# Attention scores by 64-row matmuls in pairs, with queries and keys stored whole and split on chip

## The chip, the core and the metric

One of the eight cores of a Trainium2 chip runs the whole program. The metric is the device time of one launch in microseconds. A core has a matrix engine (PE, with its weight loads, PEld, shown as an engine of their own), a vector engine (DVE), an activation engine (ACT), a general engine (POOL) and a queue that issues DMA transfers (SP). Each runs its own instructions in order and waits on semaphores for the others.

## What is computed

Two layers over a sequence of 1024 tokens of width 1024, everything in float32. Each layer is a norm, an input projection that also gives a gate, rotary embedding of queries and keys, attention, the gate, an output projection, a norm and a residual.

```python
# layer 0: three head groups of 16 heads of width 64, (window, dilation) = (128,1), (512,4), (2048,16)
qkv = (h @ w_in)[..., :n_qkv]; gate = (h @ w_in)[..., n_qkv:]
q, k = rope(q, pos), rope(k, pos)
o_g, lse_g = dilated_window_attention(q_g, k_g, v_g, window, dilation)     # for each group g
y = (sum_g softmax(lse)_g * o_g) * silu(gate) @ w_out
# layer 1: 8 heads, each with two query/key streams c of width 64 and values of width 128
s = einsum('bqhcd,bkhcd->bchqk', qblk, k) * scale                          # causal
p = softmax(s); a = p[:, 0] - lam * p[:, 1]; o = a @ v
y = (rmsnorm(o) * (1 - lambda_init)) * silu(gate) @ w_out
```

The contraction of every score, q times k, runs over the 64 elements of one head (or of one stream).

## The kernel before

**Numbers in two parts.** A float32 matrix x is held as xh (x rounded to the type float32r) and xl = x - xh. A product of two such matrices is made of xh·wh, xh·wl and xl·wh, three matmuls into one PSUM bank: `project` (L276) for the projections of queries, keys (tile `pqk`) and gates (`pg`), `v_block` (L213) for the values (`pv`), the loops of L386 and L443 for the output projection (`po`, `pe`). A PSUM bank holds 128 x 512 float32 numbers, and a matmul moves at most 512 columns.

**Order of the work.** PE takes its instructions in the order of the code. The other engines' orders are set by a scheduler from that. In each layer there is a stage that only projects, and then the attention stage. There the steps of the heads stand in a hand-made order, and a `Filler` runs matmuls of the projections between them: the remaining units of 128 queries and keys (`qk_unit`), then late gates and the first half of the output projection (`out_early`). In layer 0 the loop goes over 48 heads (8 pairs, 3 groups, 2 heads) of four steps c each: at step i come the scores of step i, the transposes of step i-3 (`tp`) and the products with the values of step i-5 (`up`), with the filler between them. In layer 1 the steps of 8 heads are sorted by due times.

**Queries and keys.** `qk_unit` projects a unit (two heads' queries and keys), applies the rotary embedding into two tiles `r`, splits each into `rh` and the rest in place (ACT rounds, POOL or DVE subtracts by `low`, L122), and stores both to DRAM (`qk_d`): four stores of 512 KB. `heads_in` then loads for one head `qh` and `ql`, each twice, into rows 0 to 63 and 64 to 127, and `ka`, whose upper 64 rows hold the keys' high part and whose lower 64 rows the low part. So one matmul over 128 rows gives qh·kh + qh·kl, and a second one ql·kh + ql·kl:

```python
for k, q in enumerate((qh, ql)):
    nc.tensor.matmul(sc[:, cols], lhsT=q[:, ts(b)], rhs=kv, start=k == 0, stop=k == 1)
```

In layer 0 (`Head.scores`, L602) step c takes the 128-query blocks 2c and 2c+1, four matmuls in one PSUM bank `sc`; a block has 128 or 256 keys. In group 0 block 0 has 128 keys and the seven others 256; in group 1 four blocks have 128 and four 256; in group 2 all have 128. In layer 1 (`DiffHead.scores`, L951) a step takes one stream s and one query block i with (i+1)·128 keys, in one or two spans of up to 512 columns, each with a bank of its own. The tag `s` of these banks has two buffers. DVE adds the mask and takes the minimum of a bank in one instruction (L609, L954), ACT takes the exponential (L612, L961). In layer 1 DVE then subtracts the second stream's probabilities from the first's (L970 to L973).

**Outputs of layer 0.** `product` adds up the values' products of four query blocks in a bank `up` (tag `u`, two buffers). When a half of the head is complete, at c = 1 and c = 3, `store` copies the lower 64 rows on ACT (`ul`, L680) and adds them to the upper ones on DVE (L685), which frees the bank. Group 2 uses `alone` instead, a bank a step.

**Loads.** In layer 0 a head's `load` (queries, keys and values `vt`) is called at c = 1 of the head before. All transfers are issued from one queue, SP, in order.

Of the kernel before, what the change touches and what calls it, by code (L numbers as in the profile page):

```python
# [18 lines left out]
P = 128  # L19
# [73 lines left out]
def trunk(ctx: ExitStack, tc: tile.TileContext, a: dict, out: bass.AP):  # L93
# [12 lines left out]
    qk_d = dram.tile([32, 2, 2, 2, 2, 32, T], F32, name="qk_d")  # L106
# [114 lines left out]
    def qk_unit(pool, unit, w, sub=1, on_pool=False):  # L221
# [7 lines left out]
        for c in range(2):  # L229
# [23 lines left out]
            latest[nc.gpsimd] = nc.gpsimd.tensor_add(put(r[1]), nat(t4), nat(t3)).ins  # L253
        written.add(unit)
        for e in range(2):
            rh = pool.tile([P, T], F32R, tag="rh", name="rh")
            nc.scalar.copy(rh, r[e])
            eng = nc.vector if on_pool or unit in (22, 23) else nc.gpsimd
            latest[eng] = low(eng, r[e].bitcast(F32R), r[e], rh).ins
            for i, t in enumerate((rh.bitcast(F32), r[e])):  # L260
                nc.sync.dma_start(qk_d[unit, :, :, i, e].rearrange("s h f t -> f (s h) t"), t)

    def heads_in(pool, unit, h):

        qh, ql, ka = (pool.tile([P, T], F32R, tag=t, name=t) for t in ("qh", "ql", "ka"))
        for t, e in ((qh, 0), (ql, 1)):
            for i in range(2):
                nc.sync.dma_start(
                    t[64 * i : 64 * i + 64].bitcast(F32), qk_d[unit, 0, h, e].rearrange("e f t -> (e f) t"))
        nc.sync.dma_start(ka.bitcast(F32), qk_d[unit, 1, h].rearrange("l e f t -> (l e f) t"))  # L270
        return qh, ql, ka
# [34 lines left out]
    def late_gates(pool, layer, w, fs, prepare):  # L306

        s = pool.tile([P, len(fs), T], F32, tag="r", name="sil", bufs=3 - layer)
        for v in gate_units(pool, layer, w, fs, None, prepare):
            if type(v) is tuple:  # L310
                f, c, o = v
                nc.scalar.copy(s[:, f - fs[0], ts(c, 512)], o)
            else:
                yield v
        nc.scalar.activation(s[:, : len(fs)], s[:, : len(fs)], AF.Silu)
        for i, f in enumerate(fs):
            nc.sync.dma_start(sil_d[layer][f], s[:, i])
            written.add(("gate", layer, f))
# [43 lines left out]
    r_bufs = {}  # L362
# [20 lines left out]
    def out_block(n, banks, kt, wh, wl, first, last):  # L383
        for c in range(2):
            for k, (l, r_) in enumerate(((XH, wh), (XH, wl), (XL, wh))):
                nc.tensor.matmul(  # L386
                    banks[c], lhsT=l[:, kt, ts(n)], rhs=r_[:, ts(c, 512)],
                    start=first and k == 0, stop=last and k == 2,
                )
                yield 512  # L390
# [23 lines left out]
    def out_weights(pool, w, kt):  # L414

        tags = {2: ("rh", "rh"), 4: ("qh", "ql"), 5: ("r", "r"), 6: ("ka", "ka")}
        if kt in tags:
            tiles = [pool.tile([P, D], F32 if t == "r" else F32R, tag=t, name="ow", bufs=2 if t != "r" else r_bufs[pool])
                     for t in tags[kt]]
            tiles = [t.bitcast(F32R) for t in tiles] if kt == 5 else tiles  # L420
        else:
            tiles = w_tiles([P, D])
        raw = raw_tile([P, D])
        nc.sync.dma_start(raw, w[ts(kt), :])
        split(*tiles, raw)
        return tiles

    def out_early(pool, layer, w, ws):

        ws[EARLY - 1] = out_weights(pool, w, EARLY - 1)  # L430
        for n in range(NB):
# [6 lines left out]
            for c in range(2):  # L438
                bank = ps.tile([P, 512], F32, tag="pj", name="pe")
                for kt in range(EARLY):  # L440
                    wh, wl = ws[kt]
                    for k, (l, r_) in enumerate(((XH, wh), (XH, wl), (XL, wh))):
                        nc.tensor.matmul(  # L443
                            bank, lhsT=l[:, kt, ts(n)], rhs=r_[:, ts(c, 512)],
# [109 lines left out]
    r_bufs[ep] = 3  # L554
    with tc.tile_pool(name="l0", bufs=2) as lp:
# [4 lines left out]
        class Head:  # L560
# [6 lines left out]
            def load(self):  # L567
                self.fin = heads_in(ep, NG * self.pr + self.g, self.h)
# [13 lines left out]

            def keys(self, b):
# [4 lines left out]
            def scores(self, c):  # L588

                qh, ql, ka = self.fin  # L590
                st = self.st
                sc = ps.tile([P, 512], F32, tag="s", name="sc")
# [542 lines left out]
```

## Time and profile before

| | |
|---|---|
| times of three runs | 1979.99, 1969.75, 1965.12 us; median 1969.75 us |
| the profiled execution | 1968.05 us, span 1966.1 us |
| layer 0, first to last score matmul | 426.6 to 1201.9 us of the span |
| layer 1, first to last score matmul | 1430.2 to 1864.6 us |
| bytes moved by DMA | 397.90 MB |
| matmuls | 10008, each with a weight load |

A row of the trace's timeline is start and length in us, engine, line, operation, output tile <- input tiles, stationary rows*columns, shape, count. A matmul's length is longer than the time until the next one starts, since matmuls are pipelined and their ends are modelled: what a matmul costs PE is the distance between starts. A weight load (PEld) belongs to the matmul that follows it.

### The profile page before, as it was taken

The page shows a single profiled execution, that of the slowest core. Times are in us where ns is not written, and L with a number is a line of the kernel's source. Part 1 is how long each engine was busy: PE and PEld are TensorE (multiplying, and loading weights), DVE is VectorE, ACT ScalarE, POOL GpSimd, SP SyncE. Part 2 cuts the span into 40 slices and gives each one's busy share as a digit, 9 for nine tenths or more (in the row PEclk, how much of TensorE's full clock was granted, in tenths as well). Part 3 has the DMA queues.
Part 4 walks back from the last instruction along what each step waited for, and adds up shares of the span by engine and source line. Part 5 has one row for each costly group of instructions (what it writes and reads, how often), then busy time and mean ns, then how long its engine had stood idle before and what let it go on. Part 6 is the DMA issues. An engine that isn't in the chain of part 4 may idle for free.

```text
span 1966.1 us, 29074 instructions
## 1 busy us (share of the span) xinstructions
PE 1885.2 (96%) x10008; PEld 1585.9 (81%) x10008; DVE 981.7 (50%) x2618; ACT 887.1 (45%) x2043; POOL 784.5 (40%) x553
## 2 busy tenths in 40 slices
PE   7999999999999999999999879999989899999897
PEld 5788888888888888888888757788878798887776
DVE  5311121135555555555555633650176778778726
ACT  4212112125656565656565645441244455556622
POOL 0000001154585857676776532320742435423201
PEclk9999999999999999999999989999999999999999
DMA  6424344277798989898989798442644565555843
GB/s 226 161 91 134 110 146 156 96 225 220 217 291 238 301 230 290 244 290 249 283 263 267 226 321 244 173 158 99 184 150 150 172 208 170 188 180 196 271 149 129
DMA packets 223683, 397.90 MB, mean 202 GB/s; under 512 B 40880, under 2 KB 131504, under 8 KB 223536
## 3 DMA queue, kind: packets, MB, share of 16 engines
q1 hardware_dynamic: 223536, 396.04, 64.2%
q8 instruction: 80, 1.31, 0.3%
q14 instruction: 67, 0.55, 0.1%
HBM read 254.87 MB, written 132.71 MB: 197 GB/s over the span
## 4 chain that ended last, share of the span: by engine, by line
PE 78%; DMA 8%; DVE 6%; ACT 2%; POOL 2%; issue 2%; SPq 1%; POOLq 0%; DVEq 0%; ACTq 0%
PE pqk L276 32%; PE pv L213 17%; PE pg L276 8%; PE po L386 4%; PE sc L602 4%; PE pe L443 3%; PE tp L625 3%; PE sc L951 3%; PE up L652 2%; PE ob L1004 2%; DMA ka<-qk_d 1%; PE tp L984 1%; DVE pm L954 1%; DVE pm L973 1%; DMA st_d<-st 1%
## 5 line engine op out<-in xcount | busy, mean ns | idle before, releaser
L276 PE MATMUL pqk<-XL,wh 128*128 128x512 f32 x1024 | 419.4, 410 | 0.0
L276 PE MATMUL pqk<-XH,wh 128*128 128x512 f32 x1024 | 408.7, 399 | 1.9 <-DVE t L252 1.9
L276 PE MATMUL pqk<-XH,wl 128*128 128x512 f32 x1024 | 409.6, 400 | 0.0
L122 POOL TENSOR_TENSOR wl<-raw,wh 128x1024 fp32r<-128x1024 f32 x59 | 141.8, 2404 | 511.2 <-ACT wh L184 507.2
L612 ACT ACTIVATE pm<-pm,st 128x128 f32<-128x128 f32 (+1 forms) x384 | 170.4, 444 | 153.1 <-DVE st L609 152.1
L276 PEld LDWEIGHTS pqk<-XH,wh 128*128 128x128 f32 x1024 | 193.7, 189 | 31.0 <-DVE t L252 2.7
L276 PEld LDWEIGHTS pqk<-XH,wl 128*128 128x128 f32 x1024 | 194.1, 190 | 27.1
L276 PEld LDWEIGHTS pqk<-XL,wh 128*128 128x128 f32 x1024 | 193.5, 189 | 27.2
L122 DVE TENSOR_TENSOR pp<-tp,pp 128x512 fp32r<-128x512 f32 (+2 forms) x192 | 104.2, 543 | 127.5 <-ACT pp L629 126.8
L184 ACT CAST wh<-raw 128x1024 fp32r<-128x1024 f32 x96 | 100.5, 1048 | 148.2 <-PE pqk L276 67.2
L213 PE MATMUL pv<-vwh,XH 128*128 128x512 f32 x384 | 153.1, 399 | 2.0 <-ACT XH L158 2.0
L213 PE MATMUL pv<-vwh,XL 128*128 128x512 f32 x384 | 153.0, 398 | 1.9 <-DVE XL L122 1.3
L213 PE MATMUL pv<-vwl,XH 128*128 128x512 f32 x384 | 152.3, 397 | 0.0
L961 ACT ACTIVATE pm<-pm,mx 128x256 f32<-128x256 f32 (+7 forms) x128 | 99.4, 776 | 115.1 <-DVE mx L960 60.2
L122 DVE TENSOR_TENSOR vs<-pv,vs 128x512 fp32r<-128x512 f32 x64 | 44.2, 691 | 202.2 <-ACT vs L517 196.2
L609 DVE CUSTOM_DVE_ANT_0 pm<-sc,masks 128x128 f32<-128x128 f32 (+1 forms) x384 | 119.2, 346 | 38.1 <-PE sc L602 37.1
L629 ACT CAST pp<-tp 128x512 fp32r<-128x512 f32 (+2 forms) x192 | 89.8, 468 | 79.4 <-PE up L652 57.9
L954 DVE CUSTOM_DVE_ANT_0 pm<-sc,md 128x512 f32<-128x512 f32 (+3 forms) x192 | 102.6, 551 | 34.4 <-PE sc L951 32.0
L251 POOL TENSOR_TENSOR r<-t 128x512 f32<-128x512 f32 x64 | 84.6, 1321 | 81.0 <-DVE t L250 79.8
L122 DVE TENSOR_TENSOR wl<-raw,wh 128x1024 fp32r<-128x1024 f32 x37 | 47.9, 1296 | 134.5 <-ACT wh L184 133.1
L517 ACT CAST vs<-pv 128x512 fp32r<-128x512 f32 x48 | 28.2, 586 | 187.8 <-PE pv L213 187.8
L602 PE MATMUL sc<-ka,qh 128*128 128x128 f32 (+1 forms) x384 | 95.3, 273 | 18.0 <-DMA ka<-qk_d 12.6
(514 smaller groups left out, 4430.2 us busy)
## 6 DMA issues: line engine op xcount, KB each, us to landing
qk_d<-rh SPq DMA_DIRECT2D x64, 512.0 KB
qk_d<-r SPq DMA_DIRECT2D x64, 512.0 KB
qh<-qk_d SPq DMA_DIRECT2D x128, 256.0 KB
ql<-qk_d SPq DMA_DIRECT2D x128, 256.0 KB
ka<-qk_d SPq DMA_DIRECT2D x64, 512.0 KB
v_d<-vs SPq DMA_DIRECT2D x48, 512.0 KB
raw<-in_dil_qk_dram SPq DMA_DIRECT2D x48, 512.0 KB
vt<-v_d SPq DMA_DIRECT2D x48, 512.0 KB
```

What stands on the lines that cost most here:

```text
L122: return eng.tensor_tensor(o, full, hi.bitcast(F32), ALU.subtract)
L184: nc.scalar.copy(wh, raw)
L213: nc.tensor.matmul(o, lhsT=l, rhs=r_, start=first and k == 0, stop=last and k == 3 * KT - 1, skip_group_check=True)
L251: nc.gpsimd.tensor_sub(put(r[0]), nat(t1), nat(t2))
L276: nc.tensor.matmul(o, lhsT=l[:, kt, :], rhs=r_[:, kt, tok], start=kt == 0 and k == 0, stop=kt == KT - 1 and k == 2)
L386: nc.tensor.matmul(banks[c], lhsT=l[:, kt, ts(n)], rhs=r_[:, ts(c, 512)], start=first and k == 0, stop=last and k == 2,)
L602: nc.tensor.matmul(sc[:, cols], lhsT=q[:, ts(b)], rhs=kv, start=k == 0, stop=k == 1)
L609: nc.vector.tensor_tensor_reduce(pm[:, cols], sc[:, cols], m[:, m.shape[1] - w_ :], 1.0, 3.0e38, ALU.add, ALU.min, st[:, 0, j : j + 1])
L612: nc.scalar.activation(pm[:, cols], pm[:, cols], AF.Exp, bias=st[:, 0, j : j + 1], scale=-1.0, accum_out=st[:, 1, j : j + 1])
L629: nc.scalar.copy(pp[:, 0, :w_], tp[:, :w_])
L954: nc.vector.tensor_tensor_reduce(pm[:, k0:k1], sc[:, :w_], m_, 1.0, 3.0e38, ALU.add, ALU.min, mx[:, j : j + 1])
L961: nc.scalar.activation(pm[:, :wq], pm[:, :wq], AF.Exp, bias=mx[:, 0:1], scale=-1.0, accum_out=den)
```

## The change

- **Storage.** `qk_unit` no longer splits. It stores the two tiles `r` as they are, two stores of 512 KB a unit.
- **Loads and splits.** In layer 0 `Head.load` loads one tile `qk` of 512 + 640 or 512 + 512 columns: rows 0 to 63 hold the first half of the head's queries and the keys that they need, rows 64 to 127 the second half and its keys. `Head.split` splits it into `qkh` and the rest in place (ACT, then POOL; DVE for the last two units). Load and split are called two heads ahead, at c = 0 and c = 2; the values are loaded one head ahead as before, by `load_values`. In layer 1 the keys `k` and two halves of the queries `q` hold stream 0 in rows 0 to 63 and stream 1 in rows 64 to 127, and are split on ACT and DVE.
- **Scores.** `row_tiled` issues three products, qh·kh, qh·kl, ql·kh, each as a pair of matmuls over 64 rows: one with rows 0 to 63 into one bank, one with rows 64 to 127 into the other. ql·kl is not computed. In layer 0 the pair is a block of the first and one of the second half of the head: step c takes blocks c and 7-c (group 0) or c and c+4. In layer 1 it is the two streams, a step is now one span of a query block for both, and the subtraction of the streams (`difference`) is put off until after the reductions of the next step.
- **Around it.** In layer 0 both halves of a head's output are complete at c = 3 only, so both stores come there; `ul` has two buffers. Tiles that later hold output weights, and the late gates' tiles, are cut anew.

```diff
+        for e in range(2):
+            nc.sync.dma_start(qk_d[unit, :, :, e].rearrange("s h f t -> f (s h) t"), r[e])
         written.add(unit)
-        for e in range(2):
-            rh = pool.tile([P, T], F32R, tag="rh", name="rh")
-            nc.scalar.copy(rh, r[e])
-            eng = nc.vector if on_pool or unit in (22, 23) else nc.gpsimd
-            latest[eng] = low(eng, r[e].bitcast(F32R), r[e], rh).ins
-            for i, t in enumerate((rh.bitcast(F32), r[e])):
-                nc.sync.dma_start(qk_d[unit, :, :, i, e].rearrange("s h f t -> f (s h) t"), t)
-
-    def heads_in(pool, unit, h):
-
-        qh, ql, ka = (pool.tile([P, T], F32R, tag=t, name=t) for t in ("qh", "ql", "ka"))
-        for t, e in ((qh, 0), (ql, 1)):
-            for i in range(2):
-                nc.sync.dma_start(
-                    t[64 * i : 64 * i + 64].bitcast(F32), qk_d[unit, 0, h, e].rearrange("e f t -> (e f) t"))
-        nc.sync.dma_start(ka.bitcast(F32), qk_d[unit, 1, h].rearrange("l e f t -> (l e f) t"))
-        return qh, ql, ka
+
+    def split_in_place(eng, hi, t):
+
+        nc.scalar.copy(hi, t.bitcast(F32))
+        low(eng, t, t.bitcast(F32), hi)
+
+    def row_tiled(outs, lq, rk):
+
+        for k, (i, j) in enumerate(((0, 0), (0, 1), (1, 0))):
+            for a, (o, q, kk) in enumerate(zip(outs, lq, rk)):
+                nc.tensor.matmul(o, lhsT=q[i], rhs=kk[j], start=k == 0, stop=k == 2)
...
             def load(self):
-                self.fin = heads_in(ep, NG * self.pr + self.g, self.h)
+
+                unit = NG * self.pr + self.g
+                self.n = 640 if self.g == 0 else 512
+                self.qk = ep.tile([P, QKW], F32R, tag="qk", name="qk", bufs=3)
+                for a in range(2):
+                    rows = self.qk[64 * a : 64 * a + 64].bitcast(F32)
+                    q, k = (qk_d[unit, s, self.h].rearrange("e f t -> (e f) t") for s in range(2))
+                    nc.sync.dma_start(rows[:, :512], q[:, ts(a, 512)])
+                    k0 = a * (T - self.n)
+                    nc.sync.dma_start(rows[:, 512 : 512 + self.n], k[:, k0 : k0 + self.n])
+
+            def split(self):
+                n = 512 + self.n
+                self.qkh = ep.tile([P, QKW], F32R, tag="qkh", name="qkh", bufs=3)
+                last = NG * self.pr + self.g in (22, 23)
+                split_in_place(nc.vector if last else nc.gpsimd, self.qkh[:, :n], self.qk[:, :n])
+
+            def load_values(self):
...
+            def blocks(self, c):
+
+                return c, 7 - c if self.g == 0 else c + 4
+
...
-                sc = ps.tile([P, 512], F32, tag="s", name="sc")
-                jobs = []
-                for b in (2 * c, 2 * c + 1):
+                jobs, ops = [], []
+                for a, b in enumerate(self.blocks(c)):
                     k0, nk = self.keys(b)
                     w_ = nk * P
-                    cols = slice(256 * (b % 2), 256 * (b % 2) + w_)
-                    kv = ka[:, k0 * P : k0 * P + w_]
-                    for k, q in enumerate((qh, ql)):
-                        nc.tensor.matmul(sc[:, cols], lhsT=q[:, ts(b)], rhs=kv, start=k == 0, stop=k == 1)
-                        cost += 256
+                    sc = ps.tile([P, 512], F32, tag="s", name="sc")
+                    rows = slice(64 * a, 64 * a + 64)
+                    at = 512 + k0 * P - a * (T - self.n)
+                    ops.append((sc[:, :w_], [t[rows, ts(b - 4 * a)] for t in (self.qkh, self.qk)],
+                                [t[rows, at : at + w_] for t in (self.qkh, self.qk)]))
+                    cost += 384
...
+                row_tiled(*zip(*ops))
+                for sc, cols, w_, j in jobs:
...
-                if c % 2:
-                    self.store(c // 2)
+                if c == 3:
+                    for half in range(2):
+                        self.store(half)
...
+        for hd in heads[:2]:
+            hd.load()
+            hd.split()
+        heads[0].load_values()
...
+                if i // 4 + 2 < len(heads):
+                    nxt = heads[i // 4 + 2]
+                    if c == 0:
+                        fill.until(NG * nxt.pr + nxt.g)
+                        nxt.load()
+                    if c == 2:
+                        nxt.split()
                 if c == 1 and i // 4 + 1 < len(heads):
-                    nxt = heads[i // 4 + 1]
-                    fill.until(NG * nxt.pr + nxt.g)
-                    nxt.load()
+                    heads[i // 4 + 1].load_values()
...
-            def load(self, part):
+            def load_keys(self):
                 fill.until(24 + self.h)
+                self.k = ep.tile([P, T], F32R, tag="k", name="k")
+                nc.sync.dma_start(self.k.bitcast(F32), qk_d[24 + self.h, 1].rearrange("h e f t -> (h e f) t"))
...
+            def split_keys(self):
+                self.kh = ep.tile([P, T], F32R, tag="kh", name="kh")
+                split_in_place(nc.vector, self.kh, self.k)
+
+            def load_queries(self, half):
+                t = ep.tile([P, 512], F32R, tag="q", name="q", bufs=3)
+                nc.sync.dma_start(
+                    t.bitcast(F32), qk_d[24 + self.h, 0].rearrange("h e f t -> (h e f) t")[:, ts(half, 512)])
+                self.q.append(t)
+
+            def split_queries(self, half):
+                self.qh.append(ep.tile([P, 512], F32R, tag="qh", name="qh", bufs=3))
+                split_in_place(nc.vector, self.qh[half], self.q[half])
...
+            def scores(self, i, j):
...
+                ops = []
+                for s in range(2):
+                    rows = slice(64 * s, 64 * s + 64)
                     sc = ps.tile([P, 512], F32, tag="s", name="sc")
-                    for k, q in enumerate((qh, ql)):
-                        nc.tensor.matmul(
-                            sc[:, :w_], lhsT=q[:, ts(i)], rhs=ka[:, k0:k1], start=k == 0, stop=k == 1)
-                    m_ = md[:, 640 - w_ :] if k1 == wq else md[:, :w_]
+                    ops.append((sc[:, :w_], [t[i // 4][rows, ts(i % 4)] for t in (self.qh, self.q)],
+                                [t[rows, k0:k1] for t in (self.kh, self.k)]))
+                row_tiled(*zip(*ops))
+                for s in range(2):
...
+                if later:
+                    later.pop()()
+                if j < len(spans) - 1:
+                    return
...
+                later.append(lambda: self.difference(i, wq, *pm, mx[1]))
+
+            def difference(self, i, wq, p0, p1, mx):
+
+                den, k = mx[:, 3:4], mx[:, 2:3]
+                nc.vector.reciprocal(den, den)
+                nc.vector.scalar_tensor_tensor(
+                    k, den, neg_lam, self.den[:, i : i + 1], ALU.mult, ALU.mult)
+                nc.vector.scalar_tensor_tensor(
+                    p0[:, :wq], p1[:, :wq], k, p0[:, :wq], ALU.mult, ALU.add)
...
-            for part in range(2):
-
-                due = h - 1 + SPAN * (NB * (NB - 1) + (part + 0.51) * NB) / 72
-                steps.append((due, lambda hd=hd, part=part: hd.load(part)))
+            for at, step in ((0.02, hd.load_keys), (0.04, lambda hd=hd: hd.load_queries(0)),
+                             (0.2, hd.split_keys), (0.22, lambda hd=hd: hd.split_queries(0)),
+                             (0.3, lambda hd=hd: hd.load_queries(1)), (0.5, lambda hd=hd: hd.split_queries(1)),
+                             (0.7, hd.load_values)):
+                steps.append((h - 1 + at, step))
-                for s in range(2):
-                    due = h + SPAN * (i * (i + 1) + (s + 0.5) * (i + 1)) / 72
-                    steps.append((due, lambda hd=hd, i=i, s=s: hd.scores(i, s)))
+                n = len(hd.spans(i))
+                for j in range(n):
+                    due = h + SPAN * (i + 1) * (i + 2 * (j + 0.25) / n) / 72
+                    steps.append((due, lambda hd=hd, i=i, j=j: hd.scores(i, j)))
+            steps.append((h + SPAN + 0.015, lambda: later and later.pop()()))
```

On PE, at the first score step of layer 0 (head 0 of group 0, blocks 0 and 1 before, 0 and 7 now), there stood:

```order
L276 MATMUL pqk<-XH,wl 128x512
L602 MATMUL sc<-ka,qh 128x128
L602 MATMUL sc<-ka,ql 128x128
L602 MATMUL sc<-ka,qh 128x256
L602 MATMUL sc<-ka,ql 128x256
L276 MATMUL pqk<-XH,wh 128x512
```

and now stands (`qkh` is the high part, `qk` the rest; queries and keys are in one tile):

```order
L272 MATMUL pqk<-XH,wl 128x512
L267 MATMUL sc<-qkh 128x128
L267 MATMUL sc<-qkh 128x256
L267 MATMUL sc<-qk,qkh 128x128
L267 MATMUL sc<-qk,qkh 128x256
L267 MATMUL sc<-qkh,qk 128x128
L267 MATMUL sc<-qkh,qk 128x256
L272 MATMUL pqk<-XH,wh 128x512
```

Four matmuls over 128 rows have become six over 64 rows, in alternating row halves; the filler's matmuls ahead and behind are the same.

On PE in layer 1, at query block 6 (896 keys, spans of 512 and 384 columns), before, where all four matmuls are of one stream:

```order
L951 MATMUL sc<-ka,qh 128x512
L951 MATMUL sc<-ka,ql 128x512
L951 MATMUL sc<-ka,qh 128x384
L951 MATMUL sc<-ka,ql 128x384
L213 MATMUL pv<-wh,XH 128x256
```

and now the step of its second span, for both streams:

```order
L267 MATMUL sc<-kh,qh 128x384 x2
L267 MATMUL sc<-k,qh 128x384 x2
L267 MATMUL sc<-kh,q 128x384 x2
L272 MATMUL pqk<-XH,wh 128x512
L272 MATMUL pqk<-XL,wh 128x512
```

Each row with x2 is a pair, the two streams in the two row halves; a step fills both banks of the tag `s` whatever its width.

On DVE in layer 0, where head 1 ends, before (L609 are the reductions of a score step, L122 with `pp` the split of transposed probabilities, L250 and L252 the rotary embedding, L685 the add of the store):

```order
L250 TENSOR_TENSOR t<-pqk,sin 128x512
L122 TENSOR_TENSOR pp<-tp,pp 128x384
L609 ISA pm,st<-sc,masks 128x128
L609 ISA st 128x1
L609 ISA pm,st<-sc,masks 128x256
L609 ISA st 128x1
L685 TENSOR_TENSOR u<-up,ul 64x512
L122 TENSOR_TENSOR pp<-tp,pp 128x384
L252 TENSOR_TENSOR t<-pqk,cos 128x512
```

and now, with the two adds L721 of one head (L644 are the reductions):

```order
L250 TENSOR_TENSOR t<-pqk,sin 128x512
L721 TENSOR_TENSOR u<-up,ul 64x512
L122 TENSOR_TENSOR pp<-tp,pp 128x256
L644 ISA pm,st<-sc,masks 128x256
L644 ISA st 128x1
L644 ISA pm,st<-sc,masks 128x256
L644 ISA st 128x1
L721 TENSOR_TENSOR u<-up,ul 64x512
L252 TENSOR_TENSOR t<-pqk,cos 128x512
```

The second add of a head now stands behind the reductions of the score step that follows the head's last product.

More of the change, by code (lines that the diff above doesn't have):

```diff
@@ L306, in late_gates @@
     def late_gates(pool, layer, w, fs, prepare):
[L308 to L312, printed above, removed]
-            else:
[L314 to L317, printed above, removed]
+        for f in fs:
+            if layer:
+                s = [pool.tile([P, 512], F32, tag="x", name="sil") for _ in range(2)]
+            else:
+                t = pool.tile([P, T], F32, tag="r", name="sil", bufs=3)
+                s = [t[:, ts(c, 512)] for c in range(2)]
+            for v in gate_units(pool, layer, w, (f,), None, prepare if f == fs[-1] else None):
+                if type(v) is tuple:
+                    nc.scalar.copy(s[v[1]], v[2])
+                else:
+                    yield v
+            for c in range(2):
+                nc.scalar.activation(s[c], s[c], AF.Silu)
+            for c in range(2):
+                nc.sync.dma_start(sil_d[layer][f, :, ts(c, 512)], s[c])
             written.add(("gate", layer, f))
@@ L414, in out_weights @@
     def out_weights(pool, w, kt):
[L416 to L422, printed above, removed]
+        spare = out_spare[pool].get(kt)
         raw = raw_tile([P, D])
         nc.sync.dma_start(raw, w[ts(kt), :])
-        split(*tiles, raw)
-        return tiles
+        halves = lambda t: [t[:, ts(c, 512)] for c in range(2)]
+        if spare is None or len(spare) == 1:
+            tiles = w_tiles([P, D]) if spare is None else spare[0]()
+            split(*tiles, raw)
+            return [halves(t) for t in tiles]
+        tiles = []
+        for c, new in enumerate(spare):
+            tiles.append(new())
+            split(*tiles[c], raw[:, ts(c, 512)])
+        return list(zip(*tiles))
     def out_early(pool, layer, w, ws):
@@ L620, in transposes @@
                 n = 0
-                for kb in (2 * c, 2 * c + 1):
+                for kb in self.blocks(c):
                     for b in (kb, kb + 1):
@@ L639, in product @@
                     self.up = [None, None]
[L642 removed]
+                for kb in self.blocks(c):
                     for half in range(2):
@@ new lines, in spans @@
+            @staticmethod
+            def spans(i):
+                wq = (i + 1) * P
+                cut = wq - max(256, wq - 512) if wq > 512 else 0
+                return [(0, cut), (cut, wq)] if cut else [(0, wq)]
+            def scores(self, i, j):
+                spans = self.spans(i)
+                wq = (i + 1) * P
+                if j == 0:
+                    self.now = (
+                        lp.tile([P, wq], F32, tag=f"pm0{i}", name="pm0", bufs=1),
+                        lp.tile([P, T], F32, tag="pm1", name="pm1"),
+                        [lp.tile([P, 4], F32, tag=f"mx{s}", name=f"mx{s}") for s in range(2)])
+                *pm, mx = self.now
+                k0, k1 = spans[j]
+                w_ = k1 - k0
+                m_ = md[:, 640 - w_ :] if k1 == wq else md[:, :w_]
+                ops = []
+                for s in range(2):
+                    rows = slice(64 * s, 64 * s + 64)
@@ L1066, in filler1 @@
             yield from out_early(ep, 1, a["diff_w_out"][0], held)
-        heads = [DiffHead(h) for h in range(8)]
+        heads, later = [DiffHead(h) for h in range(8)], []
         held = {}
```

108 lines of the change are left out of this document (48 added, 60 removed).

## The prediction

> **What bounds the kernel now.** I read the busy times first, then the same by stage, then single score steps in the timeline.
>
> ```profile
> PE 1885.2 (96%) x10008; PEld 1585.9 (81%) x10008; DVE 981.7 (50%) x2618; ACT 887.1 (45%) x2043; POOL 784.5 (40%) x553
> 1100.00:1190.00 90.00, 67.97 (x362) 56.23 (x360) 40.50 (x125) 48.34 (x125) 34.59 (x26) 0.89 0.91 274
> 440.00:1100.00 660.00, 658.81 (x3723) 562.63 (x3722) 368.15 (x1184) 388.47 (x1078) 449.17 (x312) 1.00 0.88 261
> 1420.00:1905.00 485.00, 457.00 (x2769) 400.06 (x2768) 348.77 (x953) 248.13 (x484) 178.04 (x120) 0.99 0.58 185
> ```
>
> Behind the colon stand the stretch's length, the busy time of PE, PEld, DVE, ACT and POOL, the granted clock, the DMA share and GB/s. PE leads with 96%. In 660 us of layer 0's attention it idles for 1.2 us, so whatever a score step saves or costs PE there is time of the kernel. Slack is in two places: the end of layer 0 (22 us of 90) and layer 1 (28 us of 485).
>
> A busy PE is not PE at its peak, so I look at what a score step occupies: a step of four 128-column matmuls, then one of four 256-column ones, then the 512 and 384 columns of layer 1.
>
> ```profile
> 880.01 0.22 PE L602 MATMUL sc<-ka,qh 128*128 128x128 f32 x1
> ...
> 880.13 0.19 PEld L602 LDWEIGHTS sc<-ka,qh 128*128 128x128 f32 x1
> 880.24 0.19 PEld L602 LDWEIGHTS sc<-ka,ql 128*128 128x128 f32 x1
> 880.35 0.19 PEld L276 LDWEIGHTS pqk<-XH,wh 128*128 128x128 f32 x1
> ...
> 880.69 0.39 PE L276 MATMUL pqk<-XL,wh 128*128 128x512 f32 x1
> 811.23 0.28 PE L602 MATMUL sc<-ka,qh 128*128 128x256 f32 x1
> ...
> 811.94 0.39 PE L276 MATMUL pqk<-XL,wh 128*128 128x512 f32 x1
> 1578.88 0.40 PE L951 MATMUL sc<-ka,ql 128*128 128x512 f32 x1
> 1579.11 0.34 PE L951 MATMUL sc<-ka,qh 128*128 128x384 f32 x1
> 1579.29 0.34 PE L951 MATMUL sc<-ka,ql 128*128 128x384 f32 x1
> ```
>
> A 512-column matmul holds PE for 0.23 us (1578.88 to 1579.11), a 384-column one for 0.18. The first step holds PE from 880.01 to 880.69 less the 0.23 of the 512-column matmul behind it, 0.45 us, the second in the same way 0.48. So a 256-column matmul costs 0.12, and a 128-column one hardly less, 0.11: there the weight loads set the pace, one every 0.11 us (880.13, 880.24, 880.35).
>
> **The scores, the main term.** How many there are, in layer 1 (layer 0 has 48 heads of 8 blocks):
>
> ```profile
> L951 PE MATMUL sc<-ka,qh x192: 221/386/687, 1430.2 to 1864.3; 128*128 128x512 f32 x80, 128*128 128x256 f32 x48, 128*128 128x384 f32 x48, 128*128 128x128 f32 x16
> ```
>
> By the masks, 16·(1+4+8) = 208 of layer 0's 384 blocks have 128 columns and 176 have 256, two matmuls each: 416·0.11 + 352·0.12 = 88 us. Layer 1 has the quoted row twice (for `qh` and `ql`): 160·0.23 + 96·0.18 + 96·0.12 + 32·0.11 = 69 us. Together 157 us of PE.
>
> The change makes six matmuls of four, 576 more in all, each over half the rows. If both of a pair run at once, loads included, a step takes three slots for four: 157/4 = **39 us less**. No row of this trace shows two matmuls at once; the ends are three slots (-39) and six (+78, nothing shared). I take three slots, since the two of a pair share neither rows, weights nor bank, and give what lies between to the rivals. The Trainium skill ("TensorEngine Tiling (Array Packing)", Key Properties) says that different tiles can load weights and multiply in parallel; no run here shows it yet.
>
> **Switching between full and half rows.** A step now switches PE into 64-row tiles and back: 288 steps, 576 switches. One operation of this kernel has a tile that isn't 128 by 128, the transposes `tps` with 32 columns:
>
> ```profile
> L691 PE MATMUL tps<-ident,st 128*32 128x128 f32 x8 | 2.2, 272 | 0.0
> 467.04 0.40 PE L276 MATMUL pqk<-XL,wh 128*128 128x512 f32 x1
> 467.04 0.10 PEld L691 LDWEIGHTS tps<-ident,st 128*32 128x32 f32 x1
> 467.27 0.27 PE L691 MATMUL tps<-ident,st 128*32 128x128 f32 x1
> 467.28 0.77 PEld L652 LDWEIGHTS up<-pp,vt 128*128 128x128 f32 x6
> ```
>
> Its load starts with the matmul before it, its matmul comes the usual 0.23 us later, and the six loads behind it take 0.77 - 0.19 = 0.58 us for five distances, 0.12 each. So this switch costs nothing, and I put 0 for the others. It is a narrower tile, though, not a shorter one. The upper end is what a matmul's modelled end lies behind its successor's start, 0.40 - 0.23 = 0.17 us: PE would have to run empty before it changes tiles, 576·0.17 = 98 us in all.
>
> The Trainium skill (same page and section) states a rule that speaks against this change: changing the tiling mode, not just the tile, drains TensorE. On `tps` the trace disagrees; by the rule the scores and switches together would come to about +59 us, by the row to -39.
>
> **The output banks of layer 0.** Both banks `up` of a head are now held until c = 3, and the next head's first product needs both. The add of one store of before, and the next head's products:
>
> ```profile
> 885.73 1.08 DVE L685 TENSOR_TENSOR u<-up,ul 64x512 f32<-64x512 f32 x1
> ...
> 886.55 0.57 PE L652 MATMUL up<-pp,vt 128*128 128x256 f32 x4
> ```
>
> The bank comes free at 886.81. That hurts nobody now, because the products of 886.55 go to the other bank. With two stores, and the second add behind the next step's reductions, the second bank would come free at 887.9 at the earliest, 1.1 us after the second block of that product wants it (886.55 + 0.23). Behind the waiting matmul stands all of PE. There are 32 heads of groups 0 and 1: 31 such places, 0 us where DVE is ahead, 34 where each is like this one. DVE is busy for 56% of this stretch and this place is one of its fuller ones by the order; I take a third, **+12 us**.
>
> **The score banks.** A step now takes both banks of tag `s`, so it waits for the reductions of the step before.
>
> ```profile
> 881.03 0.08 DVE L609 DVE_READ_ACCUMULATOR2_ANT st<- 128x1 f32 x1
> ...
> 884.03 0.22 PE L602 MATMUL sc<-ka,qh 128*128 128x128 f32 x1
> PE sc L951 <- DVE mx L954: 17.3, 14, 2.8
> ```
>
> In layer 0 the reductions are over 2.9 us before the next step's matmul: +3 us for those where DVE is late, up to +10. In layer 1 PE waits 17.3 us for these banks already. A step of two spans took both banks there too, and `difference` now stands behind the reductions instead of ahead of the next ones. I take 0, with ends of -17 (all gone) and +17 (twice as much).
>
> **The loads.** At the end of layer 0 the chain of waits runs through transfers:
>
> ```profile
> 1117.60 9.08 DMA vt<-v_d
> 1126.70 10.73 DMA XH<-y_d
> 1137.45 7.79 DMA wb<-wt_d
> 1145.26 8.62 DMA ka<-qk_d
> qk_d<-rh SPq DMA_DIRECT2D x64, 512.0 KB
> qk_d<-r SPq DMA_DIRECT2D x64, 512.0 KB
> qh<-qk_d SPq DMA_DIRECT2D x128, 256.0 KB
> ql<-qk_d SPq DMA_DIRECT2D x128, 256.0 KB
> ka<-qk_d SPq DMA_DIRECT2D x64, 512.0 KB
> ```
>
> SP issues in order, so the load of `ka` stands behind that of `wb`, which waits for its own data, and PE waits for `ka`. Queries and keys are now asked for two heads ahead, and their bytes fall from 64 + 96 MB (the five rows) to 32 + 34 MB, of 398 in all. Both work on the 22 idle us of that stretch; `vt` and `wb` stay as they were. I take **-12**, between 0 and -22.
>
> **Moved at no cost.** The splits keep their number of elements, but for 16 heads of 1152 columns:
>
> ```profile
> L122 POOL TENSOR_TENSOR r<-r,rh 128x1024 fp32r<-128x1024 f32 x44 | 105.5, 2406 | 4.7 <-ACT rh L257 4.7
> ```
>
> An eighth of 2.4 us more sixteen times is 5 us of POOL, busy for 449 of 660 us. The chain of store, load, ACT's rounding and POOL's 2.4 us is covered by two heads of four steps of some 4 us (880.01 to 884.03), 32 us. Without that cover, a late split stops PE for as long as it is late.
>
> **The sum.** -39 + 12 + 3 + 0 - 12 = -36. The profiled execution took 1968.05 us, 0.1% under the median of the runs shown, so 1932.
>
> **The rivals.**
> - *Loads one after another, matmuls at once.* If the two weight loads of a pair take turns at 0.11 us, a pair of up to 256 columns costs 0.22. The first pair's loads hide behind the 0.23 us matmul ahead, so a narrow step pays five loads, 0.55, instead of 0.45 or 0.48: 104·0.10 + 88·0.07 = +17 in layer 0. In layer 1 the 40 steps of 512 columns keep their gain (-0.23 each, -9), the 384-column ones gain 1 and the narrower ones lose 2: -8. That is +9 where I have -39: **1980**. For it: the loads are the pace already at 128 columns. Against it: a load fills only its own rows.
> - *A drain at each switch* (slower than before). PE runs empty ahead of the first half-row matmul of a step and again behind the last one. At 0.17 us for each of 576 switches: 1932 + 98 = **2030**. It decides the sign from 36/576 = 0.06 us a switch. Against it stands `tps`.
> - *No overlap at all*, six slots: the change doesn't do what it says. +78 for -39: **2049**. Against it: separate banks and rows.
>
> **Chances.** Forecast 0.55, with a range of its own from 1905 to 1962 by the ends of the banks and loads; loads in turn 0.18; drain 0.17 (from 0.05 to 0.17 us each, so 1961 to 2030); no overlap 0.07; something else 0.03. About 1% (20 us) is what a measurement of this kernel can tell from no change. Of the forecast's 0.55, 0.45 lies below 1950; the turns add 0.02 there: faster 0.47. Same: 0.10 of the forecast, 0.12 of the turns, 0.06 of a mild drain, 0.01: 0.29. The rest is slower, 0.24. The range runs from 1905 to 2025: it leaves out no overlap, the fuller half of the drain and a little below.
>
> **What would show it.** A pair's two matmuls starting within some hundredths of a microsecond, and a step of 128 columns holding PE for 0.33 us (right), 0.55 (loads in turn) or 0.67 (no overlap). A gap before the first half-row matmul and behind the last one (drain). PE's waits for L721 on `up` (banks), and none for queries and keys at the end of layer 0. I am wrong above all if one of the first three steps is.

## The result, and the profile after

The changed kernel takes 2068.01 us (median of four runs), the kernel before 1971.26 us: a ratio of 1.0492 with a 95% interval from 1.0461 to 1.0522. I had forecast 1932, with a range up to 2025. The profiled execution took 2067.73 us, its span 2065.9 us, 99.8 us more than before.

The engines' busy times from the page, and the stretches of the trace that the prediction showed of before (length, then PE, PEld, DVE, ACT and POOL, the granted clock, the DMA share, GB/s):

```profile
PE 1973.3 (96%) x10584; PEld 1560.3 (76%) x10584; DVE 996.6 (48%) x2626; ACT 896.0 (43%) x2061; POOL 779.4 (38%) x554
440.00:1100.00 660.00, 632.26 (x3570) 486.36 (x3568) 338.87 (x1044) 344.23 (x948) 397.90 (x273) 0.98 0.47 144
1100.00:1190.00 90.00, 86.56 (x492) 66.54 (x493) 45.35 (x139) 45.26 (x126) 55.00 (x38) 0.98 0.48 150
1420.00:1905.00 485.00, 468.03 (x2764) 380.17 (x2762) 295.62 (x793) 212.19 (x418) 185.88 (x129) 0.98 0.35 119
```

PE still has 96%, but in the 660 us of layer 0's attention it now idles for 28 us where it idled for 1.2, and the clock is 0.98. In those 660 us it does 3570 matmuls where it did 3723, though the program has 576 more: both the steps and the waits between them have grown. The stretch from 1100 to 1190 us no longer holds layer 0's end, which now comes at 1283.7 us; by the first and last score matmuls of the two traces layer 0 takes 856.9 us for 775.3, layer 1 453.4 for 434.4.

A score step of two 256-column blocks in the timeline:

```profile
889.85 0.39 PE L272 MATMUL pqk<-XL,wh 128*128 128x512 f32 x1
890.08 0.40 PE L272 MATMUL pqk<-XH,wl 128*128 128x512 f32 x1
890.40 0.19 PEld L267 LDWEIGHTS sc<-qkh 64*128 64x128 f32 x2 [0.36 <-issue]
890.40 0.39 PE L267 MATMUL sc<-qkh 64*128 64x256 f32 x2
890.63 0.28 PE L267 MATMUL sc<-qk,qkh 64*128 64x256 f32 x2
890.75 0.28 PE L267 MATMUL sc<-qkh,qk 64*128 64x256 f32 x2
890.96 0.19 PEld L272 LDWEIGHTS pqk<-XH,wh 128*128 128x128 f32 x1
890.96 0.50 PE L272 MATMUL pqk<-XH,wh 128*128 128x512 f32 x1
891.29 0.39 PE L272 MATMUL pqk<-XL,wh 128*128 128x512 f32 x1
```

Two things are to be seen. First, each row with x2 is a pair, and the second pair is gone after 0.12 us (890.63 to 890.75), which is what one 256-column matmul took before: the two of a pair do run at once. Second, four distances are too long by some 0.1 us each: the 512-column matmul ahead (890.08 to 890.40, 0.32 for 0.23), the first pair (0.23 for 0.12), the last pair (0.21 for 0.12) and the 512-column matmul behind (0.33 for 0.23). At both ends the weight load stands at the same time as its own matmul, where the load of an ordinary matmul starts with the matmul before it. From 890.08 to 891.29, less two times 0.23, the step holds PE for 0.75 us; before it was 0.48. By the median distances over all steps between 512-column matmuls it is 0.68 us at 128 columns, 0.75 at 256 and 1.10 at 512. Three slots of 0.11, 0.12 and 0.23 are 0.33, 0.36 and 0.70, so the two switches of a step cost 0.35 to 0.40 us whatever its width.

The waits of PE, those of ACT for the loaded tiles, and one of the seven changes of the head pair in the timeline, with the stretch behind it:

```profile
PE sc L267 <- DVE mx L1024: 16.7, 17, 3.2
PE sc L267 <- DVE st L644: 10.1, 9, 2.0
PE up L687 <- DVE us__7526 L708: 3.6, 1, 3.6
PE up L687 <- DVE u L721: 3.4, 4, 1.2
ACT qkh L260 <- DMA qk<-qk_d: 90.0, 44, 14.7
868.50 3.04 SPq L788 DMA_DIRECT2D wb<-wt_d  x5
871.64 0.54 SPq L587 DMA_DIRECT2D qk<-qk_d  x1
877.38 1.05 ACT L260 CAST qkh<-qk 128x1024 fp32r<-128x1024 f32 x1 [4.32 <-DMA qk<-qk_d]
881.18 0.37 ACT L707 COPY us__7526<-up 128x256 f32<-128x256 f32 x1
882.60 0.42 DVE L708 TENSOR_TENSOR us__7526<-us__7526,up 128x256 f32<-128x256 f32 x1
883.17 0.41 PE L687 MATMUL up<-pp,vt 128*128 128x128 f32 x2 [3.61 <-DVE us__7526 L708]
883.41 0.45 PE L272 MATMUL pqk<-XH,wl 128*128 128x512 f32 x1
884.04 0.63 PE L272 MATMUL pqk<-XL,wh 128*128 128x512 f32 x1
884.47 0.63 PE L272 MATMUL pqk<-XH,wl 128*128 128x512 f32 x1
883.00:887.00 4.00, 3.83 (x15) 2.66 (x16) 2.10 (x7) 1.81 (x6) 3.84 (x4) 0.60 0.42 125
```

SP issues the loads of `qk` behind five of `wb`; ACT comes to the split of that tile and stands 4.3 us for it, and the copy out of the output bank, which is behind it on ACT, comes at 881.18. DVE's add (L708), which needs the copy and frees the bank, comes at 882.60, and PE, which needs that bank, waits 3.6 us. The granted clock of the 4 us after that is 0.60, and matmuls of 512 columns are 0.43 us apart (884.04 to 884.47). The Trainium skill ("TensorE: Matmul & The Clock Gate", Part 1) says that an idle window of about 3.4 us halves the clock; the 0.60 agrees in kind. So such a wait costs more than its length. PE's list of waits has seven of this kind, 1.6 to 4.1 us each and 23.7 in all, one at each change of the pair; five of the other six also have a stretch of 3 to 7 us at a granted clock of 0.50 beside them.

### The profile page after: what moved, and what is told of

The parts are those of the page before. It is cut to its first block, busy times and chain, and to the rows that moved or that the text cites. A ratio compares the mean times of both kernels' runs of the same rounds, so it can differ in the third digit from the quotient of the medians.

```text
span 2065.9 us, 29927 instructions
## 1 busy us (share of the span) xinstructions
PE 1973.3 (96%) x10584; PEld 1560.3 (76%) x10584; DVE 996.6 (48%) x2626; ACT 896.0 (43%) x2061; POOL 779.4 (38%) x554
## 4 chain that ended last, share of the span: by engine, by line
PE 75%; DMA 8%; DVE 7%; ACT 4%; issue 2%; SPq 2%; POOL 2%; ACTq 0%; POOLq 0%; DVEq 0%
PE pqk L272 28%; PE pv L213 16%; PE pg L272 8%; PE sc L267 6%; PE po L387 4%; PE pe L446 3%; PE up L687 3%; PE tp L660 2%; DMA qk<-qk_d 2%; PE ob L1081 2%; PE tp L1061 1%; ACT pm L1036 1%; DMA qk_d<-r 1%; DMA st_d<-st 1%; ACT wh L184 1%
## 5 line engine op out<-in xcount | busy, mean ns | idle before, releaser
L272 PE MATMUL pqk<-XH,wh 128*128 128x512 f32 x1024 | 428.4, 418 | 0.0
L272 PE MATMUL pqk<-XL,wh 128*128 128x512 f32 x1024 | 425.1, 415 | 0.0
L122 POOL TENSOR_TENSOR wl<-raw,wh 128x1024 fp32r<-128x1024 f32 x60 | 143.7, 2395 | 466.3 <-ACT wh L184 465.8
L122 DVE TENSOR_TENSOR pp<-tp,pp 128x384 fp32r<-128x384 f32 (+2 forms) x192 | 104.3, 543 | 188.7 <-ACT pp L664 188.2
L122 POOL TENSOR_TENSOR qk<-qk,qkh 128x1024 fp32r<-128x1024 f32 (+1 forms) x44 | 109.6, 2493 | 111.1 <-ACT qkh L260 101.7
L122 DVE TENSOR_TENSOR vs<-pv,vs 128x512 fp32r<-128x512 f32 x64 | 44.1, 690 | 199.6 <-ACT vs L520 195.2
L644 DVE CUSTOM_DVE_ANT_0 pm<-sc,masks 128x128 f32<-128x128 f32 (+1 forms) x384 | 120.4, 347 | 22.9 <-PE sc L267 21.1
L664 ACT CAST pp<-tp 128x384 fp32r<-128x384 f32 (+2 forms) x192 | 89.6, 467 | 91.0 <-PE up L687 75.3
L687 PEld LDWEIGHTS up<-pp,vt 128*128 128x128 f32 x544 | 82.9, 192 | 41.3 <-issue 29.0
L1024 DVE CUSTOM_DVE_ANT_0 pm<-sc,md 128x512 f32<-128x512 f32 (+2 forms) x192 | 100.3, 550 | 27.0 <-PE sc L267 26.8
L687 PE MATMUL up<-pp,vt 128*128 128x256 f32 (+1 forms) x544 | 86.4, 280 | 27.1 <-DVE us__6322 L708 4.1
```

Source lines behind the costliest of these rows:

```text
L122: return eng.tensor_tensor(o, full, hi.bitcast(F32), ALU.subtract)
L272: nc.tensor.matmul(o, lhsT=l[:, kt, :], rhs=r_[:, kt, tok], start=kt == 0 and k == 0, stop=kt == KT - 1 and k == 2)
L644: nc.vector.tensor_tensor_reduce(pm[:, cols], sc, m[:, m.shape[1] - w_ :], 1.0, 3.0e38, ALU.add, ALU.min, st[:, 0, j : j + 1])
L664: nc.scalar.copy(pp[:, 0, :w_], tp[:, :w_])
L687: nc.tensor.matmul(self.up[half][:, (qs[0] - 4 * half) * P : (qs[-1] + 1 - 4 * half) * P], lhsT=self.vt[:, kb, :], rhs=self.parts[c][:, e, ...
L1024: nc.vector.tensor_tensor_reduce(pm[s][:, k0:k1], ops[s][0], m_, 1.0, 3.0e38, ALU.add, ALU.min, mx[s][:, j : j + 1])
```

## Experiments

All ratios are to the kernel before, timed beside each run.

**Are the splits late?** The split of a head was called a head later.

```diff
-                    if c == 2:
-                        nxt.split()
+                if c == 2 and 0 < i // 4 + 1 < len(heads) and i // 4 >= 1:
+                    heads[i // 4 + 1].split()
```

> Row tiling stays; a head's split moves from two heads ahead to one head ahead (c = 2), its loads stay where they are. Theory (a queue at each change of the head pair: the loads of queries and keys stand on SP behind the joint statistics, ACT reaches the split before they land and stands in order ahead of reductions and the copy that frees an output bank): the seven changes cost 6 to 8 us each beyond the other heads' 0.95 us, about 44 us in all, and go: 2068 - 44 = 2024. Rival (the two output banks, held until c = 3, stop PE there by themselves): the waits stay, 2060 to 2070.

Measured: 2078.22 us, ratio 1.0533 (1.0508 to 1.0558). My expectation failed, but the edit hadn't done what I took it for. ACT's wait is still there, and the trace has each split some 3 us behind the issue of its loads, as before the edit:

```profile
ACT qkh L260 <- DMA qk<-qk_d: 100.1, 46, 14.5
```

The scheduler, not the order of the code, places ACT's instructions. So this run decides nothing between the theories. The 10 us that it is slower than the change stay open; the order on DVE and ACT differs in many places.

The next run ties the split to an instruction of ACT:

```diff
-                    nc.scalar.activation(
+                    self.last = nc.scalar.activation(
...
+                if c == 2 and 0 < i // 4 + 1 < len(heads) and i // 4 >= 1:
+                    with tc.issue_after(hd.last):
+                        heads[i // 4 + 1].split()
```

> In the run before, moving the call of the split moved no instruction on ACT: the scheduler put it some 3 us behind its loads' issue as before. Here it is tied behind ACT's exponentials of the second step of the head before its own, so that the loads have landed 20 us earlier. Theory (ACT stands at splits for their loads, in all 90 us, and what is behind it on ACT comes late to PE): ACT's wait for these loads falls below 10 us, the changes of the head pair lose 6 us each: 2068 - 44 = 2024. Rival (the output banks held until c = 3 stop PE by themselves): ACT's wait goes, the time stays above 2055.

Measured: 2034.45 us, ratio 1.0300 (1.0272 to 1.0328), 32 us less by the spans of the profiled executions (2034.0 for 2065.9).

```profile
ACT qkh L260 <- DMA qk<-qk_d: 16.1, 2, 14.7
PE up L687 <- DVE us__11135 L708: 6.2, 1, 6.2
440.00:1100.00 660.00, 653.33 (x3748) 504.31 (x3747) 356.87 (x1094) 358.66 (x992) 426.65 (x294) 0.99 0.50 151
```

Of ACT's 90 us of waiting 16 are left, 14.7 of them at the start of the layer, and PE idles for 7 us of the 660 for 28. Of PE's seven waits at the changes of the pair, 23.7 us, one of 6.2 is left. The theory of the standing ACT holds, at 32 us rather than 44; the output banks alone don't do it.

**Is it the switch?** Row tiling alone was undone: the same tiles, banks and order, with 128 rows and two products.

```diff
-        for k, (i, j) in enumerate(((0, 0), (0, 1), (1, 0))):
+        for k, (i, j) in enumerate(((0, 0), (1, 1))):
...
-                nc.tensor.matmul(o, lhsT=q[i], rhs=kk[j], start=k == 0, stop=k == 2)
+                nc.tensor.matmul(o, lhsT=q[i], rhs=kk[j], start=k == 0, stop=k == 1)
...
-                    rows = slice(64 * a, 64 * a + 64)
+                    rows = slice(0, P)
...
-                    rows = slice(64 * s, 64 * s + 64)
+                    rows = slice(0, P)
```

> Storage, loads, splits, banks and order of the change stay; each step's six 64-row matmuls become four 128-row ones, two into each bank, as many as before the change (they sum over both halves of the tile, so the scores are other numbers; only the time is of use). Theory (each switch between 128- and 64-row tiles costs PE 0.2 us, 576 of them): steps go back from 0.68 and 0.75 us to 0.45 and 0.47 in layer 0 (-48) and by 21 us in layer 1: 2068 - 69 = 1999. Rival (switches are free, the loss is banks, splits and loads): the fourth slot comes back, +39, 2107.

Measured: 1996.70 us, ratio 1.0125 (1.0106 to 1.0144): 71.7 us less by the spans (1994.2). Four slots over 128 rows beat three slots over 64, and the steps are back at 0.45 and 0.48 us.

> Both edits: 128-row matmuls, four a step (other numbers as scores), and the split one head ahead. If both theories hold and add: 2068 - 69 - 44 = 1955, which would put the rest of the change (unsplit storage, earlier loads, two score banks a step, late stores) at -13 against the kernel before. If the two losses hide each other: 1980 to 2000.

Measured: 1992.61 us, ratio 1.0107 (1.0082 to 1.0131). Taken alone that would speak for losses that hide each other; but, as above, the later call left the splits where they were. With the tie in its place:

> The same tie, with four 128-row matmuls a step (over both halves of the tile, so other numbers as scores). Theory: 1997 - 40 = 1957, under the kernel before, which leaves the rest of the change (storage, earlier loads) as a gain of some 15 us. Rival (banks): above 1985.

Measured: 1957.43 us, ratio 0.9918 (0.9895 to 0.9940), as expected. Both losses add, and what else the change does is a small gain. A version of it with the true scores wasn't tried: 128-row products need queries and keys in both row halves, which is twice the bytes to load.

**What does the price hang on?** Two steps' half-row matmuls together halve layer 0's switches:

```diff
+                if c % 2:
+                    return
+                scs = [ps.tile([P, 512], F32, tag="s", name="sc") for _ in range(2)]
+                for u in (c, c + 1):
...
+                        sc = scs[a][:, 256 * (u % 2) : 256 * (u % 2) + w_]
...
+                    row_tiled(*zip(*ops))
```

> Row tiling stays; in layer 0 two steps' twelve half-row matmuls are issued together (two steps share the two banks, 256 columns each), so 192 switches fewer, the same number of matmuls. Theory (0.2 us a switch): -39, 2029, less or more by how the reductions, now four in a row, fall. Rival (the loss is of each half-row matmul or pair, not of the switch): no change, 2068.

Measured: 2048.05 us, ratio 1.0383 (1.0346 to 1.0419), 20 us less than the change by the medians. The profiled execution was the shortest of the four (span 2037.8, 28 us less). Twelve matmuls of 256 columns hold PE for 1.11 us, six slots of 0.12 and once 0.40: the price goes with the batch, not with the matmul. Not all of the 39 us arrives, since PE now waits for the stores:

```profile
PE up L689 <- DVE u L723: 32.6, 26, 3.7
```

This wait was 3.4 us in the change. That it grows because the reductions come four in a row and the adds of the stores behind them is argued, not shown.

> The tie and two steps' half-row matmuls together in layer 0. If the tie is worth 44 us there too: 2048 - 44 = 2004. If the output banks stop PE (it waited 33 us for them with two steps together): 2035 to 2050.

Measured: 2009.39 us, ratio 1.0179 (1.0152 to 1.0207), 39 us less than without the tie. The wait for the stores falls from 32.6 us to a third, so most of it hung on ACT as well:

```profile
PE up L689 <- DVE u L723: 11.8, 20, 2.8
```

It is the fastest version with row tiling that I ran, and still slower than before.

One more matmul of another shape went ahead of each score step of the kernel before:

```diff
+                    if b % 2 == 0:
+                        m, n = {0: (64, P), 1: (P, 64), 2: (P, 32) if self.h == 0 else (P, P)}[self.g]
+                        nc.tensor.matmul(sc[:n, cols][:, :P], lhsT=qh[:m, b * P : b * P + n], rhs=kv[:m, :P],
+                                         start=True, stop=True)
```

> The kernel before, with one more matmul of 128 columns at the head of each score step of layer 0, into columns that the step then writes anew: a tile of 64 rows x 128 columns in group 0, of 128 x 64 in group 1, of 128 x 32 in group 2's first heads, of 128 x 128 in its second ones. Theory (only a change of the tile's rows makes PE run empty, 0.2 us each way): 64 rows hold PE 0.11 + 0.41 = 0.52 us longer a step, the three others 0.11 us, in all 64 x 0.52 + 128 x 0.11 = +47, 2016. Rival (any change of the tile's size does): 0.52 for 64 and 32 columns too, +40 more, 2056.

Measured: 2006.87 us, ratio 1.0190 (1.0160 to 1.0220). A step with the 64-row matmul, and one with the 32-column matmul:

```profile
528.85 0.40 PE L276 MATMUL pqk<-XH,wl 128*128 128x512 f32 x1
529.18 0.32 PE L603 MATMUL sc<-ka,qh 64*128 64x128 f32 x1
529.43 0.38 PE L606 MATMUL sc<-ka,qh 128*128 128x256 f32 x1
529.65 0.28 PE L606 MATMUL sc<-ka,ql 128*128 128x256 f32 x1
...
597.74 0.40 PE L276 MATMUL pqk<-XH,wl 128*128 128x512 f32 x1
597.98 0.22 PE L603 MATMUL sc<-ka,qh 128*32 128x128 f32 x1
598.04 0.28 PE L606 MATMUL sc<-ka,qh 128*128 128x128 f32 x1
598.15 0.27 PE L606 MATMUL sc<-ka,ql 128*128 128x128 f32 x1
```

Ahead of the 64-row matmul stands a distance of 0.33 us, behind it come 0.25 and 0.22; at 32 columns there are 0.24, 0.06 and 0.11, as without it.

> The same with tiles of 64 rows in the upper half of the rows (group 0), of 64 rows x 64 columns (group 1), of 32 rows (group 2, first heads) and of 96 rows (second heads). Theory: each holds PE 0.52 us longer a step, whatever the height and the place, 192 x 0.52 = +100, 2069. If the price lies in the part of the rows that is left out or in the place, the four differ by more than 0.05 us a step.

Measured: 2035.03 us, ratio 1.0333 (1.0306 to 1.0361). By the median distances one such matmul adds to a step:

| tile, rows x columns | us added to a step |
|---|---|
| 64 x 128, lower or upper half | 0.45 |
| 64 x 64 | 0.40 |
| 32 x 128 | 0.46 |
| 96 x 128 | 0.11 |
| 128 x 64, 128 x 32 | 0.11 |
| 128 x 128 | 0.11 |

With these figures the first of the two runs should be 43 us over the kernel before and the second 73; beside a kernel before of 1969.12 us they were 38 and 66, and the +87 of the first run's rival is out. So a narrow tile costs its slot alone, and one of 64 rows or fewer some 0.3 us more. That 96 rows cost nothing speaks against "any change of the rows", which I had expected.

**Do pairs need to stand side by side?**

```diff
-        for k, (i, j) in enumerate(((0, 0), (0, 1), (1, 0))):
-            for a, (o, q, kk) in enumerate(zip(outs, lq, rk)):
+        for a, (o, q, kk) in enumerate(zip(outs, lq, rk)):
+            for k, (i, j) in enumerate(((0, 0), (0, 1), (1, 0))):
```

> The change with the three products of one bank before those of the other (a, a, a, b, b, b in place of a, b, a, b, a, b), all else the same. Theory (matmuls of different row halves run at once when they stand next to each other, those of one half in turn): only the third of a and the first of b meet, five slots for three: a step of 256-column blocks holds PE 0.75 + 0.24 = 0.99 us, one of 512 columns 1.09 + 0.46 = 1.55; in all 192 x 0.23 + 34 = +78 on PE, 2146. Rival (pairs are not what saves, a half-row matmul is short by itself): no change, 2068.

Measured: 2064.51 us, ratio 1.0483 (1.0456 to 1.0510): no change, and not the 2146 that I had worked out.

```profile
885.94 0.40 PE L267 MATMUL sc<-qkh 64*128 64x256 f32 x2
886.16 0.29 PE L267 MATMUL sc<-qk,qkh 64*128 64x256 f32 x2
886.28 0.29 PE L267 MATMUL sc<-qkh,qk 64*128 64x256 f32 x2
```

The program says a, a, a, b, b, b, and the trace shows three pairs a, b. A half's matmul starts when its own half is free, though two of the other half ahead of it haven't started. My rival, that a half-row matmul is simply short, gives the same time. What speaks for pairs is that each x2 row holds one matmul of each bank at one start, since each of the three products stands once for each bank.

**The rest of the change.** The earlier loads alone, by one step (the diff moves `heads_in` from c = 1 to c = 0):

> The kernel before, with the loads of a head's queries and keys called one step earlier (c = 0 of the head before, values still at c = 1); nothing else. Theory (at the end of layer 0 the load of keys stands behind that of wb on SP, 12.6 us of PE): half of it goes, -6, 1963. Rival (the queue holds them anyway): no change, 1969.

Measured: 1969.74 us, ratio 0.9983 (0.9970 to 0.9996), 3 us of 6. PE's wait for the keys didn't go:

```profile
PE sc L604 <- DMA ka<-qk_d: 16.1, 2, 8.3
```

One step isn't enough; the queue holds them: the load of `ka` at the end of layer 0 is issued at 1142.17 us where it was 1145.26, still behind four of `wb`. Then the order of layer 1, with the calls of the loads set to fit it:

```diff
-                due = h - 1 + SPAN * (NB * (NB - 1) + (part + 0.51) * NB) / 72
+                due = h - 1 + SPAN * (61.5 + part) / 72
...
-                for s in range(2):
-                    due = h + SPAN * (i * (i + 1) + (s + 0.5) * (i + 1)) / 72
-                    steps.append((due, lambda hd=hd, i=i, s=s: hd.scores(i, s)))
+                n = len(hd.spans(i))
+                for j in range(n):
+                    due = h + SPAN * (i + 1) * (i + 2 * (j + 0.25) / n) / 72
+                    steps.append((due, lambda hd=hd, i=i, j=j: hd.scores(i, j)))
```

> The kernel before with the change's order of layer 1 alone: a step is one span of both streams, the 128-row matmuls, storage and loads as before, the streams' difference taken at once. With the split tied late and 128-row matmuls layer 1 took 426 us from first to last score matmul where it took 434 before; if the order of the steps does that, 1961; if the loads, the splits or the put-off difference do it, 1969 or more.

Measured: 2030.26 us, ratio 1.0312 (1.0293 to 1.0330). It is inconclusive on the order:

```profile
PE sc L960 <- DMA ka<-qk_d: 39.3, 9, 5.6
```

Each tile has two buffers, so the next head's loads now wait until both streams' last scores: SP's longest wait for a score matmul ahead of them is 19.9 us, before 13.9. So this order can't be judged with the loads as they were.

## Why the prediction was wrong, step by step

By the profiled spans the 99.8 us are: half rows in place of 128 rows, 78.1 (2034.0 to 1955.9; 71.7 without the tie); ACT's standing, 31.9 (2065.9 to 2034.0); and all else, -10.2 (1955.9 for 1966.1).

```profile
1146.95 0.33 PE L267 MATMUL sc<-qkh 128*128 128x128 f32 x2
L267 PE MATMUL sc<-qkh x384: 221/277/415, 426.3 to 1201.6; 128*128 128x128 f32 x112, 128*128 128x256 f32 x80
L267 PE MATMUL sc<-kh,qh x192: 221/392/628, 1430.8 to 1856.1; 128*128 128x512 f32 x80, 128*128 128x256 f32 x48, 128*128 128x384 f32 x48, 128*128 128x128 f32 x16
PE sc L267 <- DVE st L644: 12.6, 9, 2.0
PE up L687 <- DVE us__10789 L708: 5.3, 1, 5.3
PE sc L267 <- DVE mx L1025: 12.6, 10, 4.0
1129.10 0.30 PE L602 MATMUL sc<-ka,qh 128*128 128x128 f32 x1 [3.89 <-DMA ka<-qk_d]
L602 PE MATMUL sc<-ka,qh x384: 218/277/522, 426.6 to 1201.7; 128*128 128x128 f32 x144, 128*128 128x256 f32 x48
PE sc L602 <- DMA ka<-qk_d: 12.6, 2, 8.7
```

The first six rows are of the kernel with 128 rows and the tie, the last three of the one before: the first score matmul of layer 0's 45th head, the first and last starts of the products with the high parts, and waits of PE.

- **The scores, -39: right.** The two of a pair run at once, loads included, and a step takes three slots for four. The rivals of loads in turn and of no overlap are out.
- **Switching, 0: wrong, and this step failed the prediction.** I took the `tps` transposes, a tile narrower by columns, as evidence for a tile shorter by rows, and said so in passing. A narrow tile is free, a short one is not. 288 steps at 0.35 to 0.40 us are 108 us (112 at 0.345, 80 at 0.395, 96 at 0.397); with -39 that is +69, and the runs gave +72 and +78. The rival named a price at each switch and nearly its size, 0.17 us for 0.17 to 0.20, and its 2030 with ACT's 32 us is 2062. That PE runs empty at a switch, as the rival has it, isn't shown: the first pair starts at 890.40, ahead of the modelled end of the matmul before it (890.08 + 0.40). The rule of the Trainium skill that I weighed ("TensorEngine Tiling (Array Packing)", Key Properties: changing the mode drains TensorE) agrees in kind with the price that the trace shows for 64 and 32 rows; for 128 x 64 and 128 x 32 no price shows.
- **Splits moved at no cost: wrong, +32.** I asked whether the split is in time for the PE that needs its result, and it is: PE's list of waits has none for a split tile. What I left out is what stands behind it on ACT while it waits for its load.
- **Output banks +12 and score banks +3: too low, and the shares wrong.** In the kernel with 128 rows and the tie the 45th head comes 720.7 us after the first (1146.95 less 426.3), before 702.5 (1129.10 less 426.6), of which 3.89 are a wait for keys: +22 without switches. In both stretches PE does some 3920 matmuls. Up to the 45th head it waits 12.6 us for the reductions, where I had 3 and at most 10, and 5.3 us once for a bank of group 2 (L708), and never for the stores (L721); before, it had 3.5 us of other waits there. These are 14 of the 22 us. Of the rest a part is the clock, 0.50 for 3.4 us at 729.2 and for 6.8 us at 1135.4, where before it was 1.00 over the whole stretch; what else there is stays open.
- **Loads -12: right in kind, at the end of the range.** From the 45th head to the last score step it is 54.7 us (1146.95 to 1201.6), before 72.6 (1129.10 to 1201.7): -18, and -22 with the 3.89 us wait for keys that ends at 1129.10. Both of PE's waits for keys there, 12.6 us, are gone.
- **Layer 1 otherwise 0: -9.** 425.3 us from the first to the last matmul with the high parts, before 434.1 (1430.2 to 1864.3). PE's waits for the score banks fall from 17.3 to 12.6 us, and 4.2 us of waits for keys are gone, which is the 9. Which part of the change did that stays open.

For the banks and loads I had +12 + 3 - 12 = +3 us, and the runs show +22 - 22 = 0. That the two sums are so close is luck: each part was off by 7 to 10 us.

## What to carry to other kernels

By these runs row tiling pays where the time saved between going into half rows and coming back exceeds 0.35 to 0.40 us; a step here saved 0.11 to 0.23, and two steps together in layer 0 at most 0.24. Count the switches first, and put half-row matmuls in batches long enough. When a transform is moved on chip, ask not only when its result is needed but what stands behind it on its engine while it waits for its data; and where a scheduler sets that order, moving the call may move nothing.

## What the runs showed of the hardware

- A switch between 128 and 64 rows costs the last matmul before it and the first one behind it some 0.1 us each (890.08 to 890.40 for 0.23 us, 890.40 to 890.63 for 0.12), a little less for a first pair of 128 columns. The weight load isn't taken ahead across the switch: it starts with its own matmul, at 890.40 and 890.96.
- 64 and 32 rows are dear between 128-row matmuls (0.40 to 0.46 us for a matmul that has 0.11 of work), 96 rows and narrow tiles are not (0.11).
- The two row halves run as if they had queues of their own: three matmuls of one half ahead in the program don't hold up the other half (885.94, three rows x2).
- A PE wait of 3.6 us was followed by 4 us at a granted clock of 0.60.
